# A planner's reckoning of accumulating transfers, a sixth place for the weights' lower parts, and activation tables loaded at other points

## The chip, the cores and the metric

The kernel runs on one core of one Trainium2 chip. The metric is the device time of one execution in microseconds (us); less is better. A core has a matrix engine (PE in the profile, with its weight loads shown apart as PEld), a vector engine (DVE), a scalar engine that evaluates activation functions (ACT), a general engine (POOL) and an engine that only issues transfers (SP). Each takes its own instructions strictly in order and waits for the others by semaphores; transfers (DMAs) run beside them in queues.

## What is computed

Two layers over 512 tokens of width 1024 in float32. The first is a conformer convolution module and a squared-ReLU MLP; the second is latent attention with 8 heads on shared keys and values, and another such MLP. Every branch has a root-mean-square norm ahead of it and one behind it.

```python
def conformer_conv(h, ...):
    u = h @ w_pw1 + b_pw1                 # 1024 -> 2048
    a, gate = jnp.split(u, 2, axis=-1)
    u = a * jax.nn.sigmoid(gate)
    u = depthwise_conv(u, w_dw, width 31, causal) + b_dw
    u = jax.nn.silu(layer_norm(u, ln_g, ln_b))
    return u @ w_pw2 + b_pw2

def squared_relu_mlp(h, w1, w2):          # 1024 -> 4096 -> 1024
    return jnp.square(jax.nn.relu(h @ w1)) @ w2

for layer in range(2):
    if layer == 1:
        k_nope, k_rope, v = mla_shared_kv(h, ...)
    hn = rms_norm(h, mix_pre_g[layer])
    m = conformer_conv(hn, ...) if layer == 0 else mla_attention(hn, ...)   # softmax of 8 heads, 64-token chunks
    h = h + rms_norm(m, mix_post_g[layer])
    f = squared_relu_mlp(rms_norm(h, ffn_pre_g[layer]), w_ff1[layer], w_ff2[layer])
    h = h + rms_norm(f, ffn_post_g[layer])
```

## The kernel before, in words

**Arithmetic.** Each large matrix product is made in three passes on PE: a weight block `raw` is split into an upper part `wh`, which ACT writes as a rounded copy, and a lower part `wl`, the remainder. The passes are upper by upper, lower by upper and upper by lower. `wl` comes about in one of two ways. For most blocks DVE subtracts (`wl = raw - wh`). For the blocks that `lo_by_dma` names (the weights of `pw1` and `pw2`, the first blocks of `ff1`, some of the last quarter of `ff2`) ACT writes `wl = -raw` in two halves, and later POOL issues an accumulating DMA that adds prepared numbers from memory onto `wl`. Accumulating DMAs from POOL also add one weight block to another (`raw += wts`) for the sums of blocks that `ff2` needs: it is computed by Strassen's scheme, seven products for each quarter. In the trace all products are `mm<-...`; the transposes that turn a residual tile `h` into the next operand are `bc<-h`.

**Stages.** In order of time: `pw1` and the convolution to about 164 us, `pw2` to about 192 us with its post-norm (statistics `stat3`, `stat4`, the updates of the residual tiles `h`, their transposes into `bc`, and scaled copies `big121`, `big123` and so on, which are the next operand), `ff1` and `ff2` of layer 0 to about 513 us, the latent projections and keys to about 585 us, scores and softmax to about 660 us, the output projection, whose post-norm falls around 720 us, and the second MLP to the end.

**What sets the order.** The program isn't written in the order in which it is issued. A planner (class `Program`) records every operation (`record`, L300), gives each a modelled duration (`cost`, L353) and each DMA a modelled time of flight (`flight`, L381), works due times backwards from the end (`due`, L405), and schedules the engines against each other, with a rank for each operation: the place in the text for PE, the due time less a bonus `early` for the others (L427). Sixteen rounds are made (`run`, L604) and the one with the shortest modelled time is issued (`issue`, L636). So every row of the trace reads L637. A number in `cost` or `flight` thus changes no instruction by itself, but the order of the instructions on each engine, and for some operations which of two engines takes them.

**Places.** On-chip tiles come from tags with a fixed number of places, [128, 1024] for the weights and [128, 512] for most others (L655 to L663). `raw`, `wh`, `wl` and the tiles in PSUM are handed out first in, first out: the n-th tile of a tag with k places waits until the last users of tile n-k are done. `big` tiles take any free place. Where the order leaves PE idle for long the planner also inserts dummy matmuls on the identity (fillers).

**Activation tables.** ACT holds one set of function tables at a time. Four loads stand in the program: ahead of the first activation, ahead of the first sigmoid of `pw1`'s gate, ahead of silu (the text has a one-element activation on the tile `warm` for this one, L1208), and ahead of the first exp of the softmax, L1497. The one-element activation at L684 stands at the start of the text and is a copy.

Of the kernel before, what the change touches and what calls it, by code (L numbers as in the profile page):

```python
# [10 lines left out]
AF = mybir.ActivationFunctionType  # L11
# [3 lines left out]
P = 128  # L15
T = 512
D = 1024
# [244 lines left out]
def _size(ap):  # L262
    n = 1
    for _, c in list(ap.ap)[1:]:
        n *= c
    return n
# [17 lines left out]
class Program:  # L284
# [68 lines left out]
    def cost(self, engine, method, kwargs, outs, ins):  # L353
        n = max([_size(a) for a in outs + ins] or [1])
        if method == "dma_start":
            return {"scalar": 380.0, "gpsimd": 900.0}.get(engine, 400.0)
        apart = {"vector": 0.77, "scalar": 0.6}.get(engine, 0.0) * n if any(
            list(a.ap)[-1][0] > 1 for a in outs + ins if _size(a) > 8
        ) else 0.0
        if engine in ("scalar", "vector") and ins and _size(ins[0]) > 8 and ins[0].ap[0][1] < P:  # L360
            apart += 120.0 if engine == "scalar" else 97.0
        if engine == "tensor":
            n = _size(outs[0])
            if ins[0].dtype == F32R:
                k = ins[0].ap[0][1]
                return max(120.0, n / 2.4 + 13.7) + (200.0 if k < P else 0.0)
            return 109.0 if method == "transpose" else max(222.0, n / 0.6 + 9)
        few = sum(_size(a) == 1 for a in ins) if n > 8 else 0
        psum = any(a.tensor.space == PSUM for a in outs + ins)
        if engine == "vector":  # L370
            wide = [a for a in ins if _size(a) > 1]
            rate = 1.042 if len(wide) > 1 or psum else 0.521
            return 68 + rate * n + 62 * few + apart
        if engine == "scalar":
            few += "accum_out" in kwargs
            return (51 if psum else 94) + 0.833 * n + 93 * few + apart
        if engine == "gpsimd":
            return 150 + 2.1 * n
        return 450.0

    def flight(self, op):  # L381

        n = max(_size(self.model(v)) for v in list(op.args) + list(op.kwargs.values()) if isinstance(v, View))
        rows = max(self.model(v).ap[0][1] for v in list(op.args) + list(op.kwargs.values()) if isinstance(v, View))
        slow = 2.03 if "accum_op" in op.kwargs else 1.0
        op.load = n * rows / P * 1.45 * slow
        op.flight = 1500.0 + op.load + (1500.0 if slow > 1 else 0.0)

    def arrival(self, op, end, state):

# [57 lines left out]
    def schedule(self, tags):  # L448
# [49 lines left out]
        def better(op, e, cost, now):  # L498

            for f, _, _, _, c, held in op.ways:  # L500
                if f != e:
                    queue = sum(o.cost for _, _, o in avail[f] if not o.done and o is not op and o.rank < op.rank)
                    done = max(clock[f], now, port[0] if held else 0.0) + queue + c
                    if done < now + cost or (c > cost and done + SLACK < op.rank):
                        return True
            return False

        def urgent(op, e, cost, now):

            if op.held > HOLD or op.cost < 200:  # L510
                return False
            return any(
                at < now + 145 and not o.done and o.cost < TINY and o.rank < op.rank for at, _, o in future[e]
            )
# [126 lines left out]
def trunk(ctx: ExitStack, tc: tile.TileContext, xT, xN, wts, vec, along, rope, cw, out):  # L641
# [3 lines left out]
    nc = Program(tc.nc)  # L645
    tags = []

    def tag(name, n, shape, where=pool, fifo=False):
        tags.append(Tag(where, name, n, shape, fifo))
        return tags[-1]  # L650

    def one(name, shape):
        return nc.tile(tag(name, 1, shape))

    RAW = tag("raw", 5, [P, D], fifo=True)  # L655
    WH = tag("wh", 5, [P, D], fifo=True)
    WL = tag("wl", 5, [P, D], fifo=True)
    BIG = tag("big", 50, [P, T])
    TMP = tag("tmp", 5, [P, T])
    MM = tag("mm", 6, [P, T], psum, fifo=True)  # L660
    BC = tag("bc", 2, [P, T], psum, fifo=True)
# [5 lines left out]
    def big(dt=F32):  # L667
        return nc.tile(BIG, dt)

# [8 lines left out]
    n = VEC["mix_pre0"] + KT  # L678
    nc.scalar.dma_start(out=vt[:, :n], in_=vec[:, :n])
    nc.sync.dma_start(out=vt[:, n:], in_=vec[:, n:])  # L680

    warm = one("warm", [P, 1])
    nc.gpsimd.memset(warm, 0.0)
    nc.scalar.activation(warm, warm, AF.Copy)  # L684

    def v(name, j):
        o = VEC[name] + j
# [38 lines left out]
    def weight(key):  # L726

        while key not in blocks:
            name, parts = USE[len(blocks)]
            i, n = BLK[parts[0][0]], _cols[BLK[parts[0][0]]]  # L730
            if name[0] in GAINS:
                blocks[name] = scaled(name, wts[i])
                continue
            raw, hi, lo = nc.tile(RAW), nc.tile(WH, F32R), nc.tile(WL, F32R)
            step = 256 if i < 2 else n
# [452 lines left out]
    for c in range(KT):  # L1188
# [5 lines left out]
        for j in T_BLOCKS:  # L1194
            if TAPS_AFTER.get(j) == c:
                n = T_BLOCKS.index(j)
# [88 lines left out]
    def mixer_out(layer, gen):  # L1285

        MF, r2 = token_blocks(), one(f"r2_{layer}", [P, TB])
        Xn = [pair() for _ in range(KT)]

        def on_half(t):  # L1290
            y, bs = prenorm(Xn, f"ffn_pre{layer}", t), HALVES[t]
            nc.vector.scalar_tensor_tensor(
                out=r2[:, bs[0] : bs[1] + 1], in0=y, scalar=1.0 / 32, in1=y, op0=ALU.mult, op1=ALU.mult
            )

        post_norm(gen(MF), MF, row(f"mix_post{layer}"), by_halves(MF, on_half), PAIRS)
        return Xn, r2

    Xn, r2 = mixer_out(0, pw2)


    F, r1 = [[None, None] for _ in range(TB)], big()
    order = nc.tile(tag("order", 1, [T, D], dram))
# [117 lines left out]
    scale = float(192**-0.5)  # L1421
# [130 lines left out]
    Xn, r2 = mixer_out(1, wo)  # L1552
# [136 lines left out]
```

## Time and profile before

| | |
|---|---|
| median of 3 runs | 1071.65 us (1070.43 to 1072.79) |
| profiled execution, its own time | 1073.97 us |
| span of that execution in the trace | 1072.2 us |
| PE busy | 1049.3 us, 98% of the span, 5294 instructions |
| DVE busy | 768.5 us, 72%, 1556 instructions |
| ACT busy | 641.6 us, 60%, 1343 instructions |
| POOL busy | 146.8 us, 14%, 168 instructions |
| 16 DMA engines, mean rate | 190 GB/s |
| mean granted PE clock | 0.996 |

The span runs from the first to the last instruction of the trace; the execution's own time is 1.8 us more. PE works almost without a gap. The first matmul starts at 4.84 us and the last at 1062.30 us; between them PE is held up for 0.4 us or more at eighteen places, for 13.6 us in all. In a timeline a row gives start, duration, engine, line, operation, output and inputs by name, the count of like instructions in a row, and in brackets how long the engine was idle ahead of it and what released it. In a table of windows each engine has its busy time and count, and `PEclk` is the clock that PE was granted (1.00 is full).

### The profile page before, as it was taken

The numbers are of one execution on the slowest core, as the hardware profiler recorded it, in microseconds if no ns is written. First come the engines' busy times: TensorE is split into PE (matmuls) and PEld (weight loads), VectorE is DVE, ScalarE is ACT, GpSimd is POOL, SyncE is SP. The second block draws the span as 40 slices with busy tenths as digits, with TensorE's granted clock in tenths as the row PEclk, the third lists the DMA queues.
The fourth block names the chain that finished last, engine by engine and source line by source line (L and its number), as shares of the span: only waits on it lengthen the run. The fifth ranks groups of instructions, "written<-read, shape, count | busy, mean of one in ns | idle before, by whom it ended". The sixth has DMA issues, their size and how long they took to land.

```text
span 1072.2 us, 15202 instructions
## 1 busy us (share of the span) xinstructions
PE 1049.3 (98%) x5294; PEld 884.5 (82%) x5294; DVE 768.5 (72%) x1556; ACT 641.6 (60%) x1343; POOL 146.8 (14%) x168
## 2 busy tenths in 40 slices
PE   8999999999999999999999999999999999999996
PEld 7888988988888888888798888889888888888884
DVE  6599993856449548778998878456564485488798
ACT  8561785956555445464767777468566555555642
POOL 1110001101001000001115434211010010000010
PEclk9999999999999999999999999999999999999998
DMA  9997777768858858659822122548688588485684
GB/s 287 314 281 214 235 199 216 184 172 242 227 143 240 244 144 233 176 159 236 211 82 63 57 89 79 177 157 199 176 235 231 142 214 256 144 239 164 188 248 118
DMA packets 67612, 204.07 MB, mean 190 GB/s; under 512 B 7632, under 2 KB 13904, under 8 KB 67536
## 3 DMA queue, kind: packets, MB, share of 16 engines
q1 hardware_dynamic: 49680, 150.15, 41.2%
q0 software_dynamic: 13536, 49.29, 25.5%
q10 hardware_dynamic: 4320, 3.68, 1.1%
q8 instruction: 41, 0.67, 0.2%
q14 instruction: 35, 0.29, 0.1%
HBM read 197.58 MB, written 5.51 MB: 189 GB/s over the span
## 4 chain that ended last, share of the span: by engine, by line
PE 79%; DVE 9%; issue 5%; DMA 4%; ACT 3%; DVEq 0%; ACTq 0%; POOLq 0%
PE mm L637 76%; DVE big L637 5%; DMA raw<-wts 3%; PE bc L637 2%; ACT big L637 2%; DVE wl L637 1%; DVE stat L637 1%; DMA wl<-wts 1%; DVE h L637 1%; ACT wh L637 1%; ACT wl L637 1%; DMA vt<-vec 0%; DVE tmp L637 0%; ACT junk L637 0%; ACT L637 0%
## 5 line engine op out<-in xcount | busy, mean ns | idle before, releaser
L637 PE MATMUL mm<-big,wh 128*128 128x512 f32 (+1 forms) x1512 | 442.3, 375 | 2.0 <-ACT wh L637 1.2
L637 PE MATMUL mm<-wh,big 128*128 128x512 f32 (+1 forms) x1216 | 376.4, 388 | 0.6 <-ACT wh L637 0.6
L637 DVE TENSOR_TENSOR wl<-raw,wh 128x512 fp32r<-128x512 f32 (+1 forms) x353 | 228.0, 684 | 129.3 <-ACT wh L637 128.4
L637 PEld LDWEIGHTS mm<-big,wh 128*128 128x128 f32 x1512 | 275.7, 189 | 54.3 <-ACT wh L637 1.5
L637 ACT ACTIVATE wh<-raw 128x512 fp32r<-128x512 f32 (+2 forms) x444 | 250.4, 611 | 108.1 <-PE mm L637 51.8
L637 PE MATMUL mm<-big,wl 128*128 128x512 f32 (+1 forms) x756 | 282.5, 374 | 0.8 <-DMA wl<-wts 0.8
L637 PEld LDWEIGHTS mm<-wh,big 128*128 128x128 f32 x1216 | 227.0, 188 | 47.6 <-ACT wh L637 1.0
L637 PE MATMUL mm<-wl,big 128*128 128x512 f32 (+1 forms) x608 | 236.5, 389 | 2.9 <-DVE wl L637 2.9
L637 PEld LDWEIGHTS mm<-big,wl 128*128 128x128 f32 x756 | 142.5, 189 | 26.9 <-DMA wl<-wts 1.0
L637 PEld LDWEIGHTS mm<-wl,big 128*128 128x128 f32 x608 | 114.5, 188 | 27.9 <-DVE wl L637 4.8
L637 POOL DMA_DIRECT2D raw<-wts x64 | 55.5, 867 | 574.1 <-DMA raw<-wts 218.7
L637 ACT ACTIVATE big<-tmp 128x256 f32<-128x256 f32 (+1 forms) x208 | 96.3, 493 | 45.6 <-DVE tmp L637 44.1
L637 ACT ACTIVATE tmp<-mm 128x512 f32<-128x512 f32 (+1 forms) x75 | 41.9, 558 | 114.5 <-PE mm L637 112.9
L637 DVE TENSOR_TENSOR big<-big,big 128x512 f32<-128x512 f32 (+3 forms) x103 | 72.2, 718 | 44.1 <-ACT big L637 43.8
L637 PE MATMUL mm<-big,big 128*128 128x256 f32 (+3 forms) x520 | 84.2, 311 | 1.4 <-DVE big L637 0.7
L637 PEld LDWEIGHTS mm<-big,big 128*128 128x128 f32 x520 | 73.0, 190 | 6.9 <-DVE big L637 1.4
L637 ACT ACTIVATE big<-mm 128x512 f32<-128x512 f32 (+5 forms) x106 | 56.0, 536 | 33.6 <-PE mm L637 32.9
L637 DVE TENSOR_TENSOR big<-tmp,big 128x512 fp32r<-128x512 f32 (+1 forms) x96 | 61.1, 640 | 11.1 <-ACT big L637 8.7
L637 DVE SCALAR_TENSOR_TENSOR big<-big,vt,big 128x512 fp32r<-128x512 f32 (+29 forms) x95 | 63.2, 730 | 5.8 <-ACT big L637 5.7
L637 DVE TENSOR_TENSOR big<-big,mm 128x512 f32<-128x512 f32 x96 | 63.6, 677 | 1.9 <-PE mm L637 1.8
L637 DVE TENSOR_TENSOR tmp<-big,big 128x512 f32<-128x512 f32 x80 | 53.4, 683 | 12.2 <-ACT big L637 12.2
L637 POOL DMA_DIRECT2D wl<-wts x30 | 26.1, 869 | 202.8 <-ACT wl L637 163.3
(89 smaller groups left out, 779.8 us busy)
## 6 DMA issues: line engine op xcount, KB each, us to landing
raw<-wts SPq DMA_DIRECT2D x222, 512.0 KB, 5.2
raw<-wts POOLq DMA_DIRECT2D x64, 512.0 KB, 8.1
wl<-wts POOLq DMA_DIRECT2D x30, 512.0 KB, 8.0
big<-cw SPq DMA_DIRECT2D x45, 256.0 KB, 6.9
big<-wts SPq DMA_DIRECT2D x12, 256.0 KB, 4.3
row<-along SPq DMA_DIRECT2D x5, 512.0 KB, 6.1
raw<-wts SPq DMA_DIRECT2D x12, 192.0 KB, 2.9
big<-xT SPq DMA_DIRECT2D x8, 256.0 KB, 4.3
```

The source lines that it names most:

```text
L637: return f(*args, **kwargs)
```

## The change

Four edits, three of them to the planner's numbers.

- `cost` gives every ACT operation on one element 1350 ns.
- `flight` adds 3500 ns to an accumulating DMA in place of 1500 ns.
- The tag `wl` has six places in place of five, `big` 48 in place of 50.
- The one-element activation at the start is a sigmoid in place of a copy, with a bonus `early` that puts it and the memset ahead of everything else on their engines; a new one-element exp on `warm` is recorded behind the conv module's post-norm. It reads one column of `r2` (four numbers per token, made by the norm ahead of the first MLP) with scale 0. Nothing reads `warm` afterwards.

```diff
@@ cost
+        if engine == "scalar" and n == 1:
+
+            return 1350.0
         if engine == "scalar":
@@ flight
-        op.flight = 1500.0 + op.load + (1500.0 if slow > 1 else 0.0)
+        op.flight = 1500.0 + op.load + (3500.0 if slow > 1 else 0.0)
@@ trunk
-    WL = tag("wl", 5, [P, D], fifo=True)
-    BIG = tag("big", 50, [P, T])
+    WL = tag("wl", 6, [P, D], fifo=True)
+    BIG = tag("big", 48, [P, T])
@@ trunk, the first activation
     warm = one("warm", [P, 1])
+    nc.early = 2e6
     nc.gpsimd.memset(warm, 0.0)
-    nc.scalar.activation(warm, warm, AF.Copy)
+    nc.scalar.activation(warm, warm, AF.Sigmoid)
+    nc.early = 0.0
@@ trunk, behind the conv module
     Xn, r2 = mixer_out(0, pw2)
 
+    nc.scalar.activation(warm, r2[:, 0:1], AF.Exp, scale=0.0)
+
```

PE carries out the same 4846 matmuls and 176 transposes on data as before; the fillers go from 20 to 15. The table loads on ACT go from four to three: ahead of the first activation, ahead of silu, and ahead of the new exp. Five operations change their engine (three subtractions for `wl` from POOL to DVE, one such subtraction and one sum from DVE to POOL). SP and POOL issue nearly the same rows in the same order. The order on PE, DVE and ACT differs in some fifteen stretches; three follow. In these rows a name such as `wl145_7418` is a tile with its running number, so the same tile has another number behind the underscore in each kernel.

The first is ACT in the post-norm of `pw2`, around 190 us. `junk,stat` rows are sums of squares for the post-norm, `big121` to `big127` the scaled copies of the transposed tokens for `ff1`, `wl25`, `wl26`, `wh25` and `wh26` weights for `ff1`. Before:

```order
L637 ACTIVATE junk0_1781,stat3_1782<-big116_1872 128x512
L637 ACTIVATE wl25_1893<-raw25_1758 128x512 x2
L637 ACTIVATE wh25_1905<-raw25_1758 128x512
L637 ACTIVATE wl26_1912<-raw26_1786 128x512
L637 ACTIVATE wh26_1919<-raw26_1786 128x512
L637 ACTIVATE wl26_1912<-raw26_1786 128x512
L637 ACTIVATE junk0_1781,stat4_1811<-big118_1889 128x512
L637 ACTIVATE wl27_1937<-raw27_1830 128x512
L637 ACTIVATE big121_1944<-bc7_1925,vt0_94 128x256
L637 ACTIVATE big125_1949<-bc8_1927,vt0_94 128x256
L637 ACTIVATE wl27_1937<-raw27_1830 128x512
L637 ACTIVATE wh25_1905<-raw25_1758 128x512
```

After:

```order
L640 ACTIVATE wl25_1836<-raw25_1752 128x512 x2
L640 ACTIVATE junk0_1767,stat3_1768<-big114_1858 128x512
L640 ACTIVATE junk0_1767,stat3_1768<-big116_1866 128x512
L640 ACTIVATE junk0_1767,stat4_1781<-big118_1898 128x512
L640 ACTIVATE wl26_1910<-raw26_1774 128x512 x2
L640 ACTIVATE wh25_1922<-raw25_1752 128x512
L640 ACTIVATE big121_1931<-bc7_1912,vt0_94 128x256
L640 ACTIVATE big125_1935<-bc8_1914,vt0_94 128x256
L640 ACTIVATE wl27_1939<-raw27_1798 128x512 x2
L640 ACTIVATE big123_1950<-bc7_1912,vt0_94 128x256
L640 ACTIVATE big127_1955<-bc8_1914,vt0_94 128x256
L640 ACTIVATE wh25_1922<-raw25_1752 128x512
```

`wl25` now stands ahead of the sums of squares. The second half of `wh25` now comes behind `big123` and `big127`, and one upper copy of `wh26` no longer stands ahead of `big121`.

The second is ACT at the first scores, around 590 to 603 us. `big410` to `big413` are scores that exp turns into weights (`wq0` is the queries' norm factor), `big421` takes a product out of PSUM, `big406` and `big408` likewise. Before:

```order
L637 ACTIVATE big406_5850<-mm143_5826 128x256
L637 ACTIVATE wh120_5858<-raw128_5717 128x384
L637 ACTIVATE big408_5866<-mm144_5848 128x256
L637 ACTIVATE wh121_5872<-raw129_5768 128x512
L637 ACTIVATE big408_5866<-mm145_5862 128x256
L637 ACTIVATE wh122_5923<-raw130_5885 128x256
L637 ACTIVATE big421_5951<-mm150_5925 32x512 x3
L637 ACT_TABLE_LOAD
L637 ACTIVATE big410_5906,stat14_5907<-big410_5906,stat14_5907,wq0_5964 128x128
L637 ACTIVATE big411_5914,stat15_5915<-big411_5914,stat15_5915,wq0_5964 128x256
L637 ACTIVATE big412_5938,stat16_5939<-big412_5938,stat16_5939,wq0_5964 128x384
L637 ACTIVATE big413_5945,stat17_5946<-big413_5945,stat17_5946,wq0_5964 128x512
```

After:

```order
L640 ACTIVATE big408_5875<-mm144_5825 128x256
L640 ACTIVATE big408_5875<-mm145_5831 128x256
L640 ACTIVATE big410_5895,stat14_5896<-big410_5895,stat14_5896,wq0_5905 128x128
L640 ACTIVATE wh122_5933<-raw130_5900 128x256
L640 ACTIVATE big411_5913,stat15_5914<-big411_5913,stat15_5914,wq0_5905 128x256
L640 ACTIVATE big412_5944,stat16_5945<-big412_5944,stat16_5945,wq0_5905 128x384
L640 ACTIVATE big413_5953,stat17_5954<-big413_5953,stat17_5954,wq0_5905 128x512
L640 ACTIVATE big421_5991<-mm150_5927 32x512 x3
```

The table load is gone from here, and the four exps stand ahead of the copies of `big421`. The load now stands between a scaled copy for `ff1` (`big155`) and the one ahead of the next block, around 209 us.

The third is ACT in the post-norm of the output projection, around 717 to 730 us; `wl145` to `wl147` are lower parts of the second MLP's first weights, each finished by an accumulating DMA from POOL. Before:

```order
L637 ACTIVATE junk0_1781,stat48_7376<-h10_1448 128x512
L637 ACTIVATE big546_7393<-bc55_7378,vt0_94 128x256
L637 ACTIVATE big550_7398<-bc56_7380,vt0_94 128x256
L637 ACTIVATE big543_7403<-mm219_7339 128x512
L637 ACTIVATE big548_7409<-bc55_7378,vt0_94 128x256
L637 ACTIVATE big552_7413<-bc56_7380,vt0_94 128x256
L637 ACTIVATE wl145_7418<-raw153_7268 128x512 x2
L637 ACTIVATE junk0_1781,stat47_7253<-big543_7403 128x512
L637 ACTIVATE big554_7439<-bc57_7424,vt0_94 128x256
L637 ACTIVATE big558_7444<-bc58_7430,vt0_94 128x256
L637 ACTIVATE wl146_7447<-raw154_7287 128x512 x2
```

After, in the same place:

```order
L640 ACTIVATE junk0_1767,stat48_7376<-h10_1450 128x512
L640 ACTIVATE big546_7393<-bc55_7378,vt0_94 128x256
L640 ACTIVATE big550_7398<-bc56_7380,vt0_94 128x256
L640 ACTIVATE big543_7403<-mm219_7339 128x512
L640 ACTIVATE big548_7409<-bc55_7378,vt0_94 128x256
L640 ACTIVATE big552_7413<-bc56_7380,vt0_94 128x256
L640 ACTIVATE wl146_7418<-raw154_7281 128x512 x2
L640 ACTIVATE junk0_1767,stat47_7274<-big543_7403 128x512
L640 ACTIVATE big554_7439<-bc57_7424,vt0_94 128x256
L640 ACTIVATE big558_7444<-bc58_7430,vt0_94 128x256
L640 ACTIVATE wl147_7447<-raw155_7287 128x512 x2
```

Each of the three copies has moved up by one block: `wl146` stands where `wl145` stood, `wl147` where `wl146` stood (before, it came eight rows behind `wl146`), and `wl145` has gone twelve rows further up, behind the statistics of `big542` and `big544`.

## Prediction

> **What bounds the kernel now.** I read the page's head and its chain first, for the engine that sets the end.
>
> ```profile
> span 1072.2 us, 15202 instructions
> PE 1049.3 (98%) x5294; PEld 884.5 (82%) x5294; DVE 768.5 (72%) x1556; ACT 641.6 (60%) x1343; POOL 146.8 (14%) x168
> PE 79%; DVE 9%; issue 5%; DMA 4%; ACT 3%; DVEq 0%; ACTq 0%; POOLq 0%
> ```
>
> PE is busy for 98% of the span and makes 79% of the chain. The change takes no matmul on data away, so all that can be won is PE's idle time, 22.9 us with the head and the tail. Next, the windows, to see where it lies (columns: stretch, length, busy time and count of PE, PEld, DVE, ACT and POOL, granted clock, DMA share, GB/s).
>
> ```profile
> 400.00:500.00 100.00, 100.00 (x439) 82.13 (x439) 79.48 (x131) 55.17 (x110) 8.29 (x10) 1.00 0.72 199
> 500.00:600.00 100.00, 94.77 (x577) 82.74 (x575) 88.66 (x213) 66.11 (x144) 28.94 (x29) 0.98 0.46 126
> 1000.00:1072.20 72.20, 61.76 (x268) 49.71 (x266) 63.48 (x136) 34.46 (x69) 6.90 (x8) 0.96 0.70 195
> ```
>
> In an MLP (400 to 500) PE has no gap at all, although ACT and DVE are far from full: what moves there costs and brings nothing. PE waits at the joints between stages, where a post-norm or a softmax has to end before the next product. So I went through PE's timeline for its stalls, and took each stall along the new order of instructions, with the durations of the old trace. Five joints matter.
>
> **A. Post-norm of `pw2`, 180 to 193 us.**
>
> ```profile
> 192.93 0.38 PE L637 MATMUL mm<-big,wh 128*128 128x256 f32 x1 [0.67 <-ACT big L637]
> ```
>
> ```profile
> 191.37 0.63 ACT L637 ACTIVATE wl<-raw 128x512 fp32r<-128x512 f32 x1
> 191.89 0.63 ACT L637 ACTIVATE wh<-raw 128x512 fp32r<-128x512 f32 x1
> 192.41 0.83 ACT L637 ACTIVATE big<-bc,vt 128x256 fp32r<-128x256 f32 x2
> ...
> 145.09 0.60 ACT L637 ACTIVATE big<-tmp,vt 128x256 fp32r<-128x256 f32 x1 [3.15 <-DVE tmp L637]
> ```
>
> ```profile
> 185.74 0.69 DVE L637 TENSOR_TENSOR big<-mm,row 128x512 f32<-128x512 f32 x1
> ```
>
> PE waits 0.67 us for `big123`, the first of the two copies at 192.41, since the copies of `wl27` and `wh25` stand ahead of them on ACT. In the new order the half of `wh25` (0.63) comes behind `big123`. With a sixth place ACT can copy `wl20` in its idle 3.15 us before 145.09, and `wl21` to `wl23` follow earlier; PE then finishes `mm34` and `mm35`, of which the post-norm's statistics are made, ten matmuls of some 0.23 us ahead of where it did: 2.3 us. On DVE the add of `big118` (0.69) leaves the chain of `stat3`. So `h` and its copies are there about 2 us earlier, and the stall goes with what follows it in the start-to-start spacing: I take **−0.9** (bounds −0.9 to 0: what is saved can't exceed the stall, and behind it PE is full to 510).
>
> **B. End of the first MLP and the latent projections, 505 to 545 us.**
>
> ```profile
> 513.46 0.62 PE L637 MATMUL mm<-wl,big 128*128 128x512 f32 x1 [1.68 <-DVE wl L637]
> ```
>
> ```profile
> 510.00:513.50 3.50, 1.50 (x5) 0.71 (x5) 3.40 (x13) 3.50 (x8) 0.58 (x2) 1.00 1.03 260
> 513.50:517.20 3.70, 3.70 (x11) 2.84 (x11) 3.67 (x9) 3.67 (x9) 1.75 (x2) 0.54 0.99 266
> 599.03:602.44 3.41, 2.23 (x14) 1.84 (x14) 2.25 (x9) 3.36 (x10) 0.07 (x1) 1.00 0.00 0
> ...
> 527.00:545.00 18.00, 17.77 (x121) 16.06 (x120) 17.77 (x38) 12.00 (x29) 0.00 (x0) 1.00 0.28 86
> ```
>
> PE waits 1.68 us for the second half of `wl106`. In the 3.50 us up to then it is busy for 1.50, and the next 3.70 us run at a clock of 0.54: eight matmuls at 0.43 in place of 0.23 us, some 1.8 us lost. The window at 599.03, with 2.23 of 3.41 busy, kept its clock. The new order sets both subtractions for `wl106` ahead of the gain products of the post-norm, so this wait ends 1.5 to 2.5 us earlier. But the products and the statistics that follow come later by these two subtractions, and behind them the updates of `h`, for whose transposes PE waits next. From 527 to 545 DVE is busy for 17.77 of 18 us: what PE wins ahead of it, it waits for there. I take **0**: gained on one side, given back on the other. The bounds are −3.0 (1.2 of the stall and the 1.8 of the clock are both kept) and +2.5 (two subtractions of some 0.7 us and a longer wait at half the clock).
>
> The Trainium skill (TensorE: Matmul & The Clock Gate, Part 1) lets the clock fall only after an idle window of some 3.4 us. In this trace it fell behind a window that was busy for 1.50 of 3.50 us, so the trace disagrees; by the page no clock would be at stake here and B would have −1.2 as its lower bound.
>
> **C. First softmax, 585 to 603 us.**
>
> ```profile
> 595.91 1.79 ACT L637 ACTIVATE big<-mm 32x512 f32<-32x512 f32 x3 [4.70 <-PE mm L637]
> 597.72 1.28 ACT L637 ACT_TABLE_LOAD   x1
> 599.02 0.49 ACT L637 ACTIVATE big<-big,stat,wq 128x128 f32<-128x128 f32 x1
> ```
>
> ```profile
> 590.29 0.98 PE L637 MATMUL mm<-big,big 128*128 128x128 f32 x6 [0.50 <-DVE big L637]
> ...
> 600.27 0.30 PE L637 MATMUL bc<-ident,big 128*128 128x128 f32 x1 [1.18 <-DVE big L637]
> ```
>
> ```profile
> 589.55 2.61 DVE L637 TENSOR_TENSOR big<-mm,big 128x512 fp32r<-128x512 f32 x6
> ...
> 596.17 0.16 DVE L637 SCALAR_TENSOR_TENSOR wq<-stat 128x4 f32<-128x4 f32 x1
> ```
>
> PE waits 1.18 us at 600.27 for weights that DVE scales right behind the first exp (599.02), and that waits for the copies of `big421` (1.79) and the table load (1.28). Both go from ahead of it: the load is made at about 209 us, and the exp now stands ahead of the copies. The load alone is worth at most 1.18 plus the pipeline's refill, 1.36 by the starts. On DVE most of the splits of six products (2.61 from 589.55) now come behind the chain that makes `wq` (596.17), so exp may start 1 to 2 us earlier still. The 0.50 at 590.29 has a cause on DVE that the new order also puts behind (`big396`, 1.5 us). I take **−2.0**: 1.36 and 0.67 by the starts. The bounds are 0 (splits that are put off become PE's next wait) and −2.5.
>
> The load's new place is between two ACT operations of `ff1`:
>
> ```profile
> 208.88 0.63 ACT L637 ACTIVATE big<-big 128x512 fp32r<-128x512 f32 x1
> ...
> 210.25 1.16 ACT L637 ACTIVATE wh<-raw 128x512 fp32r<-128x512 f32 x2 [0.75 <-PE mm L637]
> ```
>
> With its exp it takes some 1.5 us there, 0.75 of which ACT idles anyway. Behind it are queued the square at 208.88 and the copy of `wh29` at 210.25, which would be done about 0.8 us later, at 212.2; PE takes `wh29` at about 224. Cost 0; were that lead of 12 us gone, 0.8. At the start the load of the sigmoid set takes the place of the old first load, and the new activation (about 0.2) lies beside the wait for `vt`; 0 again, at worst +0.2.
>
> The Trainium skill (ScalarE: Activation LUTs, What ACT_TABLE_LOAD costs) puts a switch at 1283 ns of loading and some 1380 ns of drain. The load agrees (1.28); of a drain the rows show nothing, as the copy ends at 597.70, the load runs from 597.72 and exp starts at 599.02. By the page's 2.66 us C would be an estimated 1.4 us larger.
>
> **The rest of the attention, 603 to 700.** Two big places fewer, and moves by one or two places on DVE: **0**, bounds ±0.5; no stall there exceeds 0.9 us.
>
> **D. Start of the second MLP, 717 to 738 us.**
>
> ```profile
> 721.62 1.19 ACT L637 ACTIVATE wl<-raw 128x512 fp32r<-128x512 f32 x2
> ...
> 723.99 1.19 ACT L637 ACTIVATE wl<-raw 128x512 fp32r<-128x512 f32 x2
> ...
> 728.40 1.20 ACT L637 ACTIVATE wl<-raw 128x512 fp32r<-128x512 f32 x2
> ```
>
> ```profile
> 730.13 0.87 POOL L637 DMA_DIRECT2D wl<-wts  x1 [2.87 <-ACT wh L637]
> ```
>
> ```profile
> 738.30 0.38 PE L637 MATMUL mm<-big,wl 128*128 128x256 f32 x1 [0.76 <-DMA wl<-wts]
> ```
>
> ```profile
> wl<-wts POOLq DMA_DIRECT2D x30, 512.0 KB, 8.0
> ```
>
> PE waits for the accumulating DMA of `wl147`: copied at 728.40 to 729.60, issued at 730.13, landed 8.0 us later. In the new order the copy takes the place of `wl146`'s, at 723.99, and the issue follows at about 726; behind the DMA of `wl146` it lands at about 734, 3 us ahead of PE's need. The 0.76 goes, by the starts 1.0: **−1.0**, bounds 0 and −1.0. The 2 us reckoned more for these DMAs change no transfer; they only make the planner issue them earlier, as here.
>
> **E. The last post-norm, 1043 to 1072 us.**
>
> ```profile
> 1053.45 0.50 PE L637 MATMUL mm<-wl,big 128*128 128x512 f32 x1 [0.26 <-DVE wl L637]
> ...
> 1056.25 0.50 PE L637 MATMUL mm<-wl,big 128*128 128x512 f32 x1 [0.67 <-DVE wl L637]
> ```
>
> ```profile
> 1052.05 0.75 DVE L637 SCALAR_TENSOR_TENSOR h<-big,stat,h 128x512 f32<-128x512 f32 x1
> 1052.71 1.29 DVE L637 TENSOR_TENSOR wl<-raw,wh 128x512 fp32r<-128x512 f32 x2
> ```
>
> DVE now makes two more updates of `h` (0.75 each) and the statistics between ahead of `wl230`, so this comes some 2 us later, at 1055; PE has five matmuls of `mm306` put in before it (1.15 us) and so waits about 1.5 in place of 0.26 and 0.67 (1.3 by the starts); DVE, which carries the tail, ends 0.2 to 0.5 later. I take **+0.5**, bounds −1.3 (both stalls go) and +1.5.
>
> **Sum.** −0.9 + 0 − 2.0 + 0 − 1.0 + 0.5 = −3.4. The profiled execution took 1073.97 us, so 1070.6 under a profile; its median of three runs is 2.3 lower, 1071.65, and the same difference gives **1068.3**.
>
> **The rivals.**
> - *DVE takes it back (1070.5).* Besides B, C also ends in front of a full DVE: the subtractions for `wl118`, `wl133` and `wl137` come to it from POOL in these stretches (0.69 us for a half), and 17.77 of 18 us leave no room. Then C brings nothing and B costs 0.3: −0.9 + 0.3 + 0 − 1.0 + 0.5 = −1.1. For it: DVE at 99% from 527 on; against it: at 597 to 599 DVE waits for exp, and so for the load that goes.
> - *The clock is kept (1065.5).* PE's window before 513.5 needs only some 0.7 us more of work to reach the 2.23 that kept the clock; then B brings 1.8 and about 1 of the stall, −6.2 in all. Against it: the wait for `h` follows in the next window.
> - *Slower, by SP's queue (1074 or more).* In the new order the load of `raw119` stands ahead of that of `big336`:
>
> ```profile
> 512.26 0.33 SPq L637 DMA_DIRECT2D raw<-wts  x1
> 512.65 4.08 SPq L637 DMA_DIRECT2D big<-wts  x5
> ```
>
> ```profile
> 519.28 0.68 DVE L637 TENSOR_TENSOR big<-big,vt 128x512 f32<-128x512 f32 x1
> ```
>
> `raw119` waits for its place until 512.26, and then `big336` lands, with its like from 512.65, at about 518; DVE asks for it at 519.28. Past a lag of 1.2 us every further one is paid in full, as DVE is full there. Slower by 0.2% needs a lag of 6.8 us: 1.2, the 3.4 won elsewhere and 2.2. Against it: the place comes free by `wh106` and `wl106`, which move ahead.
> - *It does nothing (1071.5).* The new order only moves stalls about within each joint, and the load was hidden behind `big421`'s copies. The rows of C speak against it.
>
> **How the numbers follow.** A run tells about 0.2% (2.1 us) from no change. Forecast 0.50 (with its terms' moderate spread 1066.8 to 1069.5), DVE takes it back 0.22, the clock is kept 0.14, nothing 0.06, slower 0.08. Faster is 0.50 + 0.14 = 0.64, within 0.2% 0.22 + 0.06 = 0.28, slower 0.08. The range runs from 1064.6 (the clock kept with C at its lower end) to 1071.9 (nothing changed): it leaves out the slower case and one in ten of the rest. All bounds at once would reach −9 and +4.5; that all fall to one side I leave out.
>
> **What would show it.** A: no stall at the first matmul on `big123`. B: the granted clock between 513 and 521, and PE's next wait for `h`. C: no table load at 597, the first exp by 597 and no wait of more than 0.3 us at the transposes of the weights. D: the last of three accumulating DMAs lands before 736. E: a stall of about 1.5 us at `wl230`. The sum is wrong if DVE's stretch from 527 to 545 starts no earlier but ends later, or if a stall of over 1 us shows in a place where there was none, above all at `big336`.

## The result and the profile after

| | before | changed |
|---|---|---|
| median, in pairs on the same chip | 1071.34 us (1070.43 to 1072.79, 6 runs) | 1064.28 us (1063.41 to 1068.46, 6 runs) |
| profiled execution, its own time | 1073.97 us | 1068.46 us |
| its span | 1072.2 us | 1066.7 us |

The ratio is 0.9939 (95% interval 0.9922 to 0.9956), 7.1 us less; the forecast was 1068.3 and its lower end 1064.6. The profiled execution is the slowest of the six; the spans of the other five are 1061.6 to 1063.3. So below, a second profile of each kernel (e1 and e5) is read beside the first.

The head of the changed kernel's page, and its row for the accumulating DMAs (count, size, median from issue to landing):

```profile
span 1066.7 us, 15181 instructions
PE 1045.5 (98%) x5284; PEld 884.7 (83%) x5284; DVE 764.1 (72%) x1559; ACT 640.9 (60%) x1343; POOL 141.6 (13%) x165
...
wl<-wts POOLq DMA_DIRECT2D x30, 512.0 KB, 8.4
```

The windows of the changed kernel, same profile:

```profile
400.00:500.00 100.00, 100.00 (x439) 82.19 (x438) 80.27 (x132) 56.05 (x113) 7.77 (x9) 1.00 0.74 211
500.00:600.00 100.00, 97.35 (x594) 85.57 (x593) 92.84 (x226) 67.78 (x151) 27.76 (x30) 1.00 0.47 131
63.00:73.00 10.00, 6.31 (x30) 5.92 (x29) 10.00 (x16) 7.04 (x14) 2.59 (x3) 0.66 0.88 226
```

The MLP is full as before. From 500 to 600 PE is busy for 97.35 us in place of 94.77, at a full clock. But there is a hole where there was none: from 63 to 73 PE is busy for 6.31 of 10 us at a clock of 0.66. PE's waits in the changed kernel (total, times, longest) name it:

```profile
PE mm L640 <- DMA uu<-dealt: 3.7, 1, 3.7
PE mm L640 <- DVE big L640: 1.8, 3, 0.7
PE mm L640 <- POOL big L640: 1.6, 1, 1.6
PE bc L640 <- DVE big L640: 1.5, 3, 0.7
PE mm L640 <- ACT wh L640: 1.2, 1, 1.2
```

The waits for `wl` from DVE (four, 2.9 us in the profile of before), for `wl<-wts` (0.8) and for `big` from ACT (1.4) are gone. The first row is new: in the convolution PE waits 3.7 us for `uu`, four gathers (`uu<-dealt`) of the gated values that were written to memory as `dealt`.

To find the gain by stage I lined up the traces by the k-th matmul or transpose on data, and took the growth of the difference in start times over each stretch, against the second profile of before (e5, span 1068.0). This table is worked out from all start times, and so is every figure "by the starts" below; times at the left are e5's, figures in us, and less than 0 is a gain on e5. "flight" is the 2 us edit alone, "places" the edit of the tags, "tables" that of the activations.

| stage | before, 1st | changed, 1st | changed, 2nd (e1) | e4 | e6 | flight e7 | places e8 | tables e9 | places+flight e10 |
|---|---|---|---|---|---|---|---|---|---|
| 6 to 20, start | -1.2 | -1.4 | -1.1 | -0.3 | -0.9 | -0.9 | -1.0 | -0.4 | -0.6 |
| 61 to 72, `uu` | 0 | +6.7 | +1.7 | +4.1 | 0 | +1.8 | 0 | 0 | +1.3 |
| 130 to 150, end of convolution | -0.2 | +0.3 | +0.6 | +0.1 | +0.2 | +0.1 | +1.4 | +1.7 | +3.5 |
| 150 to 230, A | 0 | -1.3 | -1.3 | -1.3 | 0 | +0.7 | -1.5 | +0.1 | -1.5 |
| 230 to 300 | -0.7 | -0.7 | -0.7 | -0.7 | -0.6 | -0.7 | -0.5 | -0.7 | +0.2 |
| 500 to 531, B's first half | +4.9 | +0.8 | +0.6 | +1.7 | +2.1 | +0.2 | +2.0 | +1.5 | +2.3 |
| 531 to 582, B's second half | 0 | -1.5 | -1.5 | -1.5 | 0 | +1.0 | -1.1 | -1.6 | -1.6 |
| 582 to 608, C | 0 | -0.9 | -0.9 | -0.9 | -1.3 | +1.4 | +0.4 | +0.4 | -1.3 |
| 608 to 690, attention | 0 | -1.4 | -1.4 | -1.4 | 0 | -0.4 | -1.4 | -1.1 | -0.6 |
| 725 to 760, D | -0.2 | -1.6 | -1.7 | +0.5 | +0.4 | +0.5 | -1.7 | -0.1 | -1.5 |
| 760 to 1030 | +0.2 | -0.6 | 0 | -0.2 | +0.6 | -0.8 | +0.1 | +0.9 | +0.1 |
| 1030 to 1058, E | +1.5 | 0 | 0 | 0 | +1.2 | +2.0 | +0.3 | +0.2 | +0.1 |
| all, with the stretches left out | +4.2 | -1.4 | -5.6 | +0.2 | +1.6 | +4.7 | -2.4 | +0.9 | +0.8 |

Two executions of one program differ by up to 5 us in a place: before by 4.9 in B and 1.5 in E, the changed kernel by 5.0 at `uu`. And four of these profiles are of the slowest execution of their kernel: the changed kernel's first, e4's, e9's and above all e10's, which at 1070.72 us lies 5.7 above its median.

### The profile page after: what moved, and what is told of

Read it like the earlier page. It is cut to its first block, busy times and chain, and to the rows that moved or that the text cites. A ratio compares the mean times of both kernels' runs of the same rounds, so it can differ in the third digit from the quotient of the medians.

```text
span 1066.7 us, 15181 instructions
## 1 busy us (share of the span) xinstructions
PE 1045.5 (98%) x5284; PEld 884.7 (83%) x5284; DVE 764.1 (72%) x1559; ACT 640.9 (60%) x1343; POOL 141.6 (13%) x165
## 5 line engine op out<-in xcount | busy, mean ns | idle before, releaser
L640 PEld LDWEIGHTS mm<-big,wl 128*128 128x128 f32 x756 | 142.6, 189 | 25.7 <-DVE wl L640 0.5
L640 DVE TENSOR_TENSOR big<-big,big 128x512 f32<-128x512 f32 (+4 forms) x103 | 69.8, 698 | 55.9 <-ACT big L640 55.6
```

Source lines behind the costliest of these rows:

```text
L640: return f(*args, **kwargs)
```

## The experiments

Each time is a median, with the ratio to runs of before in between and its 95% interval. The medians of before beside them were 1071.0 to 1071.4.

### What is the wait for `uu`, and does it stay?

**e1**, the changed kernel once more.

> The changed kernel once more, for a second profile. In the first profile PE waits 3.69 us at 67.3 us for the gathers uu<-dealt, and runs at half the clock for 6.83 us behind it; the span was 1066.7, the five other executions had spans of 1061.6 to 1063.3. Theory: the wait for uu is in every execution, since the third and fourth gather are issued only when the loads of raw14 and raw15 have landed (58.30 and 62.18, issues at 58.32 and 62.20); only the half clock behind it comes and goes. Then PE again idles 2 to 4 us ahead of the first uu matmul, the clock stays at 1.00 there, and the span is about 1062. Rival: the wait itself was an accident of that execution. Then no wait over 0.5 us there, and the same span.

**e2**, the changed kernel's order, but the write of the first `dealt` and its four gathers go through POOL's queue:

```diff
         span, sequence, places = best
+        # operations 347 to 351: dealt0 and its four gathers
+        sequence = ["gpsimd" as the engine of 347 to 351; 348 to 351 ahead of 614, wl11's accumulating DMA]
```

> The changed kernel's own order, with the write of dealt and the four gathers uu<-dealt of the first block (and no other instruction) issued by POOL in place of ACT, so that they share completion semaphores with no weight load on SP. dealt's data are ready at 44.75, its DMA was issued at 49.18 when big31 had landed (49.11). Theory 1: the wait at 67 goes and what it cost stays won: dealt at 45, uu issued from about 51, landed by 58 to 60, PE starts on uu at 63.4 without a wait; total 3 to 4 us below the changed kernel. Theory 2: the joint at 513 us is set by weight loads and accumulating DMAs (in the first profile they landed 1 to 2 us later than before while PE came 6 us later); then what is won at 67 is waited for at 506 to 513, the stall of before (3.2 us and a half clock spell) is back in part, and the total falls by less than 1.5 us.

e1 took 1064.32 us, e2 1064.74 us (1064.51 to 1065.67), ratio 0.9945 (0.9930 to 0.9959). First the changed kernel's own profile: PE, then ACT with its DMA queue (`ACTq`), then SP, each from the timeline.

```profile
63.22 0.39 PE L640 MATMUL mm<-big,wh 128*128 128x512 f32 x1
67.30 6.90 PE L640 MATMUL mm<-uu,big 128*128 128x128 f32 x35 [3.69 <-DMA uu<-dealt]
```

```profile
49.18 0.33 ACTq L640 DMA_DIRECT2D dealt<-big  x1
...
55.99 6.52 ACTq L640 DMA_DIRECT2D uu<-dealt  x4
62.55 0.63 ACT L640 ACTIVATE wh<-raw 128x512 fp32r<-128x512 f32 x1 [8.56 <-DMA raw<-wts]
```

```profile
58.32 0.31 ACTq L640 DMA_DIRECT2D uu<-dealt  x1
...
62.20 0.31 ACTq L640 DMA_DIRECT2D uu<-dealt  x1
```

```profile
48.52 0.33 SPq L640 DMA_DIRECT2D raw<-wts  x1
...
51.84 0.33 SPq L640 DMA_DIRECT2D raw<-wts  x1
```

The four gathers take 6.52 us to issue, in before 1.94 (from 54.49, with no wait on PE). The third goes out at 58.32 and the fourth at 62.20. The program's list shows what the fourth waits for (a name such as `DMAHW1_49` is one of eight completion semaphores that the DMAs of SP and ACT take in turn):

```
ACT   uu00_109<-dealt0_529 32x4x128    [waits DMAHW3_49,DMAHW0_49]
ACT   uu00_109<-dealt0_529 32x4x128    [waits DMAHW5_49]
ACT   uu00_109<-dealt0_529 32x4x128    [waits DMAHW7_49]
ACT   uu00_109<-dealt0_529 32x4x128    [waits DMAHW1_49]
SP    raw14_686<-wts 128x1024          [waits DMAHW7_49,Activation_49]
SP    raw15_736<-wts 128x1024          [waits DMAHW1_49,Activation_49]
```

The third and the fourth gather share semaphores with `raw14` and `raw15`, and only go out when these weights have landed, although nothing in the data ties them together. `raw14`, issued at 48.52, took 9.8 us, so it landed at 58.3; the view of `raw15`, issued at 51.84, gives 10.3 us, so 62.2:

```profile
DMA to landing us min/median/max: 10.3/10.3/10.3
```

Both times are the gathers' issue times. In before the gathers stand at other numbers in the turn (`DMAHW1`, `3`, `4`, `6`), whose last users had landed. ACT's own next copy, of `wh11`, needs neither of these weights, but it is queued behind the gathers, and ACT stood idle for 8.56 us ahead of it.

The Trainium skill (DMA: Bandwidth & Descriptors, Anatomy of one DMA) says that a DMA engine waits for no semaphore; the engine that issues the DMA does, ahead of it. The trace agrees: the fourth gather is issued 0.02 us behind the landing of `raw15`, and ACT does nothing else meanwhile.

The size of the wait isn't fixed. In e1:

```profile
65.28 4.93 PE L640 MATMUL mm<-uu,big 128*128 128x128 f32 x42 [1.46 <-DMA uu<-dealt]
```

The same wait is 1.46 us there, 2.2 us shorter, for the fourth gather goes out at 59.92, and 1.39 in a third profile (e11). The rest of what the first profile lost is the clock. Windows of the first profile, and below of e1:

```profile
63.00:67.30 4.30, 0.61 (x4) 0.21 (x2) 4.30 (x7) 4.30 (x9) 0.95 (x2) 0.88 0.80 250
66.26:73.09 6.83, 5.79 (x27) 5.83 (x28) 6.83 (x11) 3.77 (x8) 1.73 (x2) 0.50 0.96 236
```

```profile
63.00:67.30 4.30, 2.85 (x22) 2.41 (x21) 4.30 (x7) 4.30 (x10) 1.86 (x3) 1.00 0.88 239
```

With 0.61 of 4.30 us busy PE ran at half the clock for the next 6.83 us. The longer wait and this clock are why the first profile loses 6.7 us in this stage and e1 1.7. With 2.85 of 4.30 it kept its clock.

In e2 the gathers take no turn with the loads, and POOL's queue issues them in 2.23 us:

```profile
46.46 0.58 POOL L654 DMA_DIRECT2D dealt<-big  x1 [10.18 <-DVE big L654]
...
52.69 2.23 POOL L654 DMA_DIRECT2D uu<-dealt  x4 [4.05 <-DMA dealt<-big]
```

PE then starts on `uu` without a wait, at 64.86; the mechanism is shown. The total did not follow. **e11** and **e12** timed both side by side:

> The changed kernel in the same job, to be held against the next one: 1064 to 1065 us, with the wait of 1.5 to 4 us ahead of the first uu matmul.

> The changed kernel's order with dealt and the four gathers of the first block issued by POOL, timed beside the changed kernel. Theory: the 1.7 us of waiting for uu (more where the half clock follows) are gone and stay won: 1.5 to 2.5 us below the changed kernel. Rival: in its first profile the last output DMA took 3.2 us in place of 2.1 and the tail was 1.4 us longer; if that belongs to this kernel, the total is within 1 us of the changed kernel.

The changed kernel 1064.24 us (0.9931, 0.9916 to 0.9947), with POOL 1064.96 (0.9939, 0.9924 to 0.9954): not faster. The stall of B did not come back either (+0.6 us in e2 and e12). What is won at `uu` is lost behind PE: from the start of its last matmul to the end of the span e2 and e12 take 11.4 us, the twelve other profiles 9.9 to 10.5. The last of the eight output writes shows most of it, in e2 and then in e1:

```profile
DMA to landing us min/median/max: 3.2/3.2/3.2
```

```profile
DMA to landing us min/median/max: 2.1/2.1/2.1
```

It takes 3.2 us in e12 too, and 2.05 to 2.08 in every profile but these two. (Writes of 2.9 us in e3 and 4.6 in e7 are earlier ones, which hold up nothing.) So the loss comes with the edit in both of its profiles; why the last write lands later with it stays open, and no version here beat the changed kernel.

### Is it the table load that C won by?

**e3**, the changed kernel without the one-element exp, so that the load falls back to the first exp of the softmax. **e6**, the kernel before in its own order, with that exp added behind `big155`:

```diff
# e3, changed kernel
         span, sequence, places = best
+        sequence = [e for e in sequence if e[0] is None or e[0].n not in {1575}]
# e6, kernel before; i: the copy into big155, w: warm
+        sequence.insert(i + 1, (None, ("scalar", "activation", (w, w, AF.Exp), {})))
```

> The changed kernel's own order without the one-element exp, so that the table load falls back ahead of the softmax's first exp; nothing else moves. Theory: the load stands on the path there: first exp and PE's transposes 1.3 us later, total +1.0 to +1.4. Rival: the new order gives ACT idle time ahead of the first exp (wq comes from DVE), the load hides in it: total within 0.4.

> The kernel before, its own order kept instruction by instruction, with a one-element exp (warm to warm) put in on ACT behind big155 at 208.8 us, so that the exp table is loaded there. Theory: in the order of before the load stands on the path to the first exp; PE's wait at 600.27 falls from 1.36 to about 0.1 and the total by 1.0 to 1.4 us. Rival: something else, the scores' scaling on DVE or the copies of big421, ends as late; total within 0.4 us of before. The wait of PE at 210 to 225 stays zero by both.

e3 took 1064.80 us (0.9946, 0.9930 to 0.9963): as fast as with the exp. e6 took 1071.01 us (0.9992, 0.9974 to 1.0010), no measurable change in all (the interval has room for the 1.3 us and for none), though stage C is 1.27 us shorter. ACT in e3, then in e1:

```profile
587.06 1.28 ACT L641 ACT_TABLE_LOAD   x1
589.83 0.49 ACT L641 ACTIVATE big<-big,stat,wq 128x128 f32<-128x128 f32 x1 [1.49 <-DVE stat L641]
```

```profile
589.82 0.50 ACT L640 ACTIVATE big<-big,stat,wq 128x128 f32<-128x128 f32 x1 [2.78 <-DVE stat L640]
```

In the new order ACT waits 2.78 us for `stat` ahead of the first exp, and the load fits into it: exp starts at 589.83 with it and at 589.82 without. C gains 0.9 us in both. In the old order, where exp stands behind the copies of `big421`, the load was on the path, and e6 shows its price:

```profile
209.69 1.28 ACT L643 ACT_TABLE_LOAD   x1
210.99 0.20 ACT L643 ACTIVATE warm<-warm 128x1 f32<-128x1 f32 x1
...
594.01 1.79 ACT L643 ACTIVATE big<-mm 32x512 f32<-32x512 f32 x3 [5.14 <-PE mm L643]
595.83 0.50 ACT L643 ACTIVATE big<-big,stat,wq 128x128 f32<-128x128 f32 x1
```

Exp follows the copies at once, and the stage is 1.27 us shorter, the 1.28 of the load. By the Trainium skill (ScalarE: Activation LUTs, What ACT_TABLE_LOAD costs), which puts a switch with its drain at 2.66 us, an estimated 2.66 us would have been won; no drain shows here either. At 209 the load costs nothing, as forecast: e6's stages from 150 to 230 differ by 0.0.

### Was it the sixth place that won D?

**e4**, the changed kernel with the copies for `wl145` to `wl147` and their accumulating DMAs back behind the operations that they followed in before:

```diff
+MOVES = [([5932, 5934, 5936], 5753, 1), ([5964, 5966, 5968], 5767, 1), ([5996, 5998, 6000], 5837, 1)]
         span, sequence, places = best
+        for ns, at, behind in MOVES: [take ns out of sequence and put them behind at]
```

> The changed kernel's own order with the copies of wl145, wl146 and wl147 and their accumulating DMAs back at the places of before (behind big552, big558 and the second sum of squares of stat47). Theory: the third DMA again lands 0.8 to 1.1 us after PE asks for it, and that is the price: total +0.8 to +1.2. Rival: something else ends just behind it, total within 0.4.

1067.56 us (0.9967, 0.9955 to 0.9978): 3.3 us of the gain are lost, where 0.8 to 1.2 were expected. PE and POOL in e4, then POOL in e1:

```profile
734.36 1.06 PE L653 MATMUL bc<-ident,h 128*128 128x128 f32 x8 [1.19 <-DVE big L653]
735.18 0.48 PE L653 MATMUL mm<-big,wh 128*128 128x256 f32 x2
736.45 0.38 PE L653 MATMUL mm<-big,wl 128*128 128x256 f32 x1 [0.79 <-DMA wl<-wts]
```

```profile
727.38 0.87 POOL L653 DMA_DIRECT2D wl<-wts  x1 [3.10 <-ACT wh L653]
```

```profile
717.13 0.88 POOL L640 DMA_DIRECT2D wl<-wts  x1 [15.45 <-ACT big L640]
719.07 0.87 POOL L640 DMA_DIRECT2D wl<-wts  x1 [1.06 <-ACT big L640]
```

The wait for `wl<-wts` is back at 0.79 us (0.76 in before), and D is 2.1 us longer than in e1. By the starts this wait makes up 1.0 of it. The other 1.0 is new: with the late copies in this order ACT also hands `big` to DVE later (DVE waits 1.22 us for it, in e1 0.18), and PE waits 1.19 us for the transposes, where neither before nor the changed kernel has a wait. In e1 the last of these DMAs goes out at 719.07, 8.3 us ahead of e4's; 3.9 of that is e4's lag at this point, so the place in the order is worth 4.4. So D is the order's, as forecast. The profile is of the slowest of e4's ten executions (1070.14), and shows two more losses against e1: the first matmul on `uu` (+2.4, here with a wait of 2.19 for the last load of `cw`) and B (+1.1), stages that vary from one execution to the next. They are not put down to the edit, and the other 1.2 us of the median's loss stay open.

### Is before itself steady, and which edit does it?

**e5**, the kernel before once more.

> The kernel before once more, for a second profile: its first one had a span of 1072.2 us, thirteen later executions 1067.9 to 1070.8. Theory 1: the waits of 3.2 us at 510 to 513.5 are in every execution, and the half clock behind them (1.8 us) comes only where the free-running window falls so; then this profile shows the waits, a clock of 1.00 from 513 to 517 and a span of 1068 to 1071. Theory 2: the half clock is always there; then it shows again, and the difference to the first profile lies elsewhere.

It took 1069.81 us. In the place of B's stall:

```profile
510.00:513.50 3.50, 3.50 (x17) 2.88 (x16) 3.46 (x12) 3.50 (x8) 1.75 (x2) 1.00 1.08 269
```

PE is busy for 3.50 of 3.50 us, where the first profile had 1.50: no wait, no lower clock, in the same program. The stall on which part B was argued is there in some executions and not in others, as are the two at the end (E).

**e7** to **e10** make the edits singly or in a pair; each is planned anew. e7: only the 3500 in `flight`. e8: only the two tags. e9: only the activations with their cost. e10: tags and `flight`.

> The kernel before with only the 2 us more reckoned for an accumulating DMA; the planner makes its order anew. Theory (the wait at 510 to 513 comes from accumulating DMAs that are issued late: raw114's lands at 507.71, wh106 and wl106 are made from it): reckoned longer, they are issued earlier, the waits at 510 to 513 and at 738 go, total -4 to -6. Rival: the sixth place is what frees the weights earlier; then this edit alone leaves most of the wait at 513, total -1 or less. The table load at the first softmax stays (1.3 there).

> The kernel before with only the sixth place for wl and 48 big tiles in place of 50; the planner makes its order anew. Theory: the sixth place alone brings the copies of wl ahead in the post-norms, so the waits at 193 and 738 go (-0.9 and -1.0) and the wait for uu at 65 appears (+1.6); the waits at 510 to 513 stay, since the accumulating DMAs are reckoned as before: total -1 to +1. Rival: the sixth place is what shortens the ring of weights at 510; total -4 to -6.

> The kernel before with only the table edits (1350 ns reckoned for an ACT operation on one element, sigmoid first, the exp ahead of ff1); the planner makes its order anew. Theory: the first softmax gains about 1.3 as it did with the old order kept (PE's wait at 597 to 600 gone), nothing else changes its cause: accumulating DMA of raw108 issued as late as before (23 to 25 us ahead of PE's matmul at 500), so the wait at 510 to 513 still comes in some executions; the waits at 193 and 738 stay. Total -1 to -2. Rival: the load is worth nothing in any new order; total within 1 of before.

> The change without the table edits (sixth place, 48 big tiles, 2 us more for accumulating DMAs); the planner makes its order anew. Theory: these two carry the change: the sixth place takes away the waits at 193 and 738 (-1.3 and -1.7), the 2 us bring raw108's accumulating DMA to 27 us ahead of PE and keep the wait at 513 away; total -5 to -8, like the change, with the wait for uu at 65 (+1.7) in it. Rival: the order is chaotic and the gain needs all three; total -3 or less.

| | median us | ratio (95%) |
|---|---|---|
| e7, flight | 1074.92 | 1.0018 (1.0001 to 1.0035) |
| e8, places | 1067.88 | 0.9968 (0.9952 to 0.9984) |
| e9, tables | 1069.96 | 0.9985 (0.9972 to 0.9998) |
| e10, places and flight | 1064.99 | 0.9944 (0.9926 to 0.9963) |
| all (e11) | 1064.24 | 0.9931 (0.9916 to 0.9947) |

The edits don't add up, and what e7 and e8 were expected to take was missed by theory and rival alike. `flight` alone costs 3.5 us by the medians and 1.9 by the ratio (its ten times stand in two groups, around 1072.4 and 1075.2), yet put upon the two tags it brings 2.9 (1067.88 to 1064.99). The table by stage shows why it loses alone: against e5 the planner's new order is worse at C (+1.4), E (+2.0), `uu` (+1.8), B's second half (+1.0) and A (+0.7). The wait for `uu` is there with the `flight` edit (e7, e10, all) and not without it (e8, e9): it comes from the place that the gathers happen to have in the turn of the semaphores. A and D come with the sixth place (e8, e10) and not without it (e7, e9). The table edits bring nothing at C in the order that they lead to by themselves (e9, +0.4), although they take the load away: the theory that C is the load fell a second time.

## Why the prediction was right or wrong

**The side was right** and the time 4.0 us too high: the median lies 0.3 us below the range. That end of the range was itself added up wrongly: the rival's 1065.5 less the 0.5 of C gives 1065.0, not 1064.6 (and eight matmuls that lose 0.20 us each are 1.6 us, not 1.8). The steps that failed are B, the rest of the attention, E and C's main term. That the total came as near as it did is partly luck: a loss at `uu` that the prediction did not look for stands against gains that it put at nothing. By its steps:

- **A, -0.9: right, small by 0.4.** No wait is left at `big123`, and the stage gains 1.3 us in every profile of the changed order. The bound "what is saved can't exceed the stall" failed; the other 0.4 lies in pieces too small for a row of waits.
- **B, 0: the step failed.** "Gained on one side, given back on the other" rested on a stall of one execution and on a DVE that leaves no room from 527 to 545. The stall comes and goes in before (+4.9, 0, +2.1 us in three profiles) and is nearly gone in the changed kernel (+0.6 to +1.0 in six, +1.7 in e4): on the average some 1.5 us less. And nothing is given back: from 531 to 582 the changed kernel wins 1.5 us. Before had ten dummy matmuls there (first row), which are no longer planned, but they can't be most of it: e9 (second row) still has eight of them and wins 1.6 us, and in the 3 us around them (540 to 543) the changed kernel wins 0.5. The rest is spread (0.6 from 531 to 534, 0.4 from 570 to 582), and what makes it stays open.

```profile
541.71 1.27 PE L637 MATMUL bc<-ident 128*128 128x128 f32 x10
```

```profile
541.27 1.05 PE L640 MATMUL bc<-ident 128*128 128x128 f32 x8
```

  The first wait goes with the 2 us edit. PE's wait for `wl` from DVE (0.49 to 1.68 us, between 512 and 514) is in four of the five profiles without that edit, all but e5, and in none of the nine with it (e7, e10 and seven in the changed kernel's order). The sixth place is not what takes it away, for e8 has it:

```profile
513.31 0.50 PE L637 MATMUL mm<-wl,big 128*128 128x512 f32 x1 [1.55 <-DVE wl L637]
```

  With the edit the first accumulating DMA of a `raw` block behind 455 us is issued 25.1 to 25.7 us ahead of the matmul that starts at 500 in e5, without it 20.8 to 23.2. That this lead is what does it is not shown: among the five without the edit, e5 with 21.8 has no wait and e6 with 23.2 has one. e4 and e10, which have the edit, wait for `h` a little later (0.86 and 1.58 us).
- **C, -2.0: right in sign, and its main term fell.** 0.9 us were won, and none of it by the load (e3). What moved is the exp, ahead of the copies of `big421`; that this wins the 0.9 was not tried by itself. The 1.36 for the load would have been right in the old order (e6, 1.27). A wait of 0.74 us for `big` from DVE, foreseen as a bound ("splits that are put off") now stands at 587.54 in e1.
- **The rest of the attention, 0: the step failed.** It gains 1.4 us, nearly all of it from 640 to 690. In before its three waits of 0.58, 0.39 and 0.38 us are in that stretch; in the changed kernel two are left, 0.25 and 0.60. By the starts the three cost 0.8, 0.6 and 0.6 us and the two cost 0.5 and 0.6, so the waits make up 0.9 of the 1.4. "Moves by one or two places on DVE" were put at nothing, and which of them took the waits away is not shown.
- **D, -1.0: right, small by 0.65** (-1.65 in six of the seven profiles of the changed order). e4 shows the mechanism. By the starts the place of the wait for `wl` itself gains 1.1 us; the rest lies in pieces of 0.2 and less. The further wait that e4 has for the transposes is not part of this, for before does not have it.
- **E, +0.5: the step failed.** No wait shows at `wl230`, where 1.5 us were foreseen. DVE in the changed kernel:

```profile
1039.47 2.49 DVE L640 TENSOR_TENSOR wl<-raw,wh 128x512 fp32r<-128x512 f32 x4
...
1046.80 0.75 DVE L640 SCALAR_TENSOR_TENSOR h<-big,stat,h 128x512 f32<-128x512 f32 x1
...
1048.86 1.29 DVE L640 TENSOR_TENSOR wl<-raw,wh 128x512 fp32r<-128x512 f32 x2
```

`wl230` starts 7.8 us ahead of the last matmul (1056.69). In before it was 9.6, and 8.9 without the 0.67 of waiting that lay between. So it came 1.1 us later and not 2, because four halves of earlier subtractions end by 1042; and PE asks 1.15 us later, as reckoned. E is a gain of some 0.7 us on the average, as before's waits come in two of three profiles (the changed order still loses 0.7 us there in one of seven, e11).

- **Missed: `uu`, +1.6 us, 6.7 in the first profile and 4.1 in e4.** The forecast named a wait in a new place as what would make it wrong, and looked for it at `big336` behind SP's queue, where none came. I followed the order on each engine, and not the semaphores that DMAs of two queues share.

The sum that the runs show: `uu` +1.6, end of the convolution +0.5, A -1.3, B -1.5 and -1.5, C -0.9, attention -1.4, D -1.65, E -0.7, together -6.85, measured -7.1. B's and E's share are means over few profiles and good to a microsecond, and the stretches left out come to another -0.7 or so, most of it from 760 to 1030.

Of the rivals, *DVE takes it back* fell (the stretch from 531 on gains). *The clock is kept* came nearest in time (1065.5), and its mechanism holds in part: the half clock at 513 is gone in the changed kernel, but two of before's three profiles (e5 and e6, which has before's order) have none there either. *Slower, by SP's queue* and *it does nothing* fell.

## What to carry to other kernels

A stall that one profile shows is a term of the sum only if a second profile of the same kernel shows it; here 5 us of "stalls" lay in one execution and not in the next. When an order is replanned, count the DMAs that share completion semaphores as well as the instructions on each engine, for a small urgent transfer may come to stand behind a large one to which no data ties it. And a long operation that is moved off a path is worth its length only in the order in which it was on the path: try it in the old order and in the new one.

## What the runs showed of the hardware

- Two 512 KB loads that took 9.8 and 10.3 us held back gathers on another engine's queue through shared completion semaphores: the fourth went out 6.2 us behind the first, in before 1.4.
- The clock fell to 0.50 for 6.83 us behind a window in which PE was busy for 0.61 of 4.30 us, and held at 1.00 behind one with 2.85 of 4.30.
- The last output write took 3.2 us from issue to landing in both profiles of the POOL version and 2.05 to 2.08 in the twelve others.
